# Order edges for the context norm and the second silu row, two more load buffers in the attention, and context rows seven pieces apart

## The chip, the cores and the metric

The kernel runs on one core of a Trainium2 chip. The core has engines that run at the same time, each through its own list of instructions in order: TensorE (PE in the profile; PEld are its weight loads) multiplies matrices, VectorE (DVE) and ScalarE (ACT) work elementwise, GpSimd (POOL) and SyncE (SP) here mostly start DMA transfers. Transfers run on 16 DMA engines; an engine that starts one goes on at once, and whoever needs the data waits for a semaphore. The metric is the device time of one execution in microseconds (us); lower is better.

## The reference

The kernel computes one block of a diffusion backbone: 512 latent tokens (SEQ) and 256 context tokens, width 2048, everything in fp32. Cut to what matters:

```python
shift, scale, gate       = split(silu(c)     @ w_ada + b_ada)      # for the latent tokens
shift_c, scale_c, gate_c = split(silu(c_ctx) @ w_ada + b_ada)      # for the context tokens
h  = rmsnorm(x,   norm_g) * (1 + scale)   + shift                  # 512 x 2048
hc = rmsnorm(ctx, norm_g) * (1 + scale_c) + shift_c                # 256 x 2048
p  = h @ w_in                                                      # 2048 x 9216: q, k, v, z_a, u_b, z_b, g_a, g_b
kc, vc = heads of hc @ w_in[:, k and v columns]
q, k = rope(rmsnorm(q)) * scale, rope(rmsnorm(k));  kc = rmsnorm(kc)
attn = softmax(q @ [k, kc].T) @ [v, vc]                            # 12 query heads, 4 key heads of 128
y_a  = (attn * silu(z_a)) @ w_proj_a                               # branch A
y_b  = (fourier_mix(u_b) * silu(z_b)) @ w_proj_b                   # branch B
y    = (sigmoid(g_a) * y_a + sigmoid(g_b) * y_b) @ w_out
out  = rmsnorm(x + gate * y, final_g)
```

The context needs a norm over its own rows (256 numbers), a scale and a shift per column, and only then its products with the key and value weights. The gate column of the conditioning, silu(c) @ w_ada, is only used at the very end.

## The kernel before

**Tiling.** Weights come from HBM in pieces of 128x1024 fp32 (512 KB), by DMAs that SyncE starts (L212) into "raw" buffers, tiles named wr. Some products use a sum of weight pieces; GpSimd builds those by accumulating loads into longer-lived chain buffers named R (L215, L280). TensorE multiplies in a reduced fp32 format; to keep precision, each piece is split in two, and every product is three matmuls, hi x hi, hi x lo and lo x hi (`mm3`, L324 to L328). The split is a copy on ScalarE (L176, tiles whi) and a subtraction on VectorE (L177, tiles wlo); smaller splits write tiles named s. Three matmuls by four make the work of one piece, twelve matmuls of 512 columns.

**Stages.** After the norm and the conditioning come eight groups of projections (g = 0 to 7: three for q and z_a, two of gates, one for k and v, two of gates). Each is done with seven products instead of eight, in a Strassen-like scheme, named in the order P1, Q5, P2, Q6, P7, Q3, Q4, with four weight pieces each. The results of products stand in PSUM under the names x, y and banks. Then comes the attention, 48 steps (12 heads by four blocks of 128 queries) plus three that run out. In each step TensorE computes scores, VectorE takes the row maximum (L1274), ScalarE the exponential (L1276), TensorE turns the probabilities (L1292) and multiplies them with the values. Branch B's products run between these as a "filler", with weight pieces called pab. GpSimd meanwhile builds sums of branch weights (`weight_sum`, from L1410 on). Branch A and the output projection follow.

**Buffers.** There are four raw buffers (`RAW`, pool `wp`), and up to two more in pool `rp` and two in pool `gvp` at times; the list `raw_pools` says which pools a load may use, and `load_more` starts loads, in order, as long as one is free. The two of `gvp` lie over an older area, the tile qr, in which normalised and rotated queries and keys are put together before they are stored (qz_d at L976, k_d at L986); the context norm's diagonals, the context rows and their forms (`cparts`, stored in cf_d) use the same tile. Whoever writes that area waits until the stores that read it are done. In the attention, tiles of 128x1024 (probabilities, queries and others) come from a list of 32 freed slots, by `take` and `give`.

**The context.** In groups 3 and 4 the pieces carry extra work, by the number n, which counts pieces from group 3 on: `context_piece` (L72) says at which n the squares of the context tokens ("cn") and a context row ("cr", `context_row`) are done. The `context_norm` (L1055) is one of the jobs called after a piece; it makes two diagonal matrices of the inverse norms (L1060), and `context_spread` (L1063), three jobs later, spreads them over the partitions with a matmul and copies them into qr (L1066). Each of the four rows multiplies its tokens with gain and norm on VectorE (L1075), forms sums (L1078, L1084) and stores them (cf_d).

**The conditioning's gate.** The row silu(c) is made in two halves (`load_row`, `silu_of_row`): a tanh on ScalarE (L1101) into a scratch tile e, then one VectorE operation (L1102). `use_gate` (L1107) multiplies 32 pieces of gate weights with it, each in a raw buffer that is free again afterwards. The first half of the row serves gates 0 to 15, the second 16 to 31; gates from number 16 on are all used in the attention.

**What sets the order.** The program is written in one sequence, and a scheduler of the tile framework puts each engine's instructions in an order from dependencies and its own estimates. `tc.issue_after(i)` adds an edge: what is issued under it stands behind instruction i. Nothing else fixes where a small operation without such an edge stands among the splits on ScalarE and VectorE.

Of the kernel before, what the change touches and what calls it, by code (L numbers as in the profile page):

```python
# [10 lines left out]
F32 = mybir.dt.float32  # L11
F32R = mybir.dt.float32r
ACT = mybir.ActivationFunctionType
ALU = mybir.AluOpType
# [4 lines left out]
P = 128  # L19
# [8 lines left out]
NKEY = T + C  # L28
# [37 lines left out]
NQZ, KV = 3, 5  # L66
# [6 lines left out]
def context_piece(g, name, pc):  # L73

    n = 28 * (g - NQZ) + 4 * ONE_GROUP.index(name) + pc
    if n % 2 == 0 and 0 <= n < 8:
        return "cn", n // 2
    if n % 8 == 2 and 18 <= n < 50:
        return "cr", n // 8 - 2

# [37 lines left out]
def block_kernel(ctx, tc, xT, ctx_rows, ctx_toks, x, c_row, w_ss, w_gate, vecs, qkg, rope, dft_c, dft_s,  # L120
                 w_start, w_g, w_pab, w_o, final_g, out):
    nc = tc.nc
# [29 lines left out]
    def uid(s):  # L152
        cnt[0] += 1
        return f"{s}{cnt[0]}"
# [25 lines left out]
    todo, ahead = [], []  # L180
    chain, left = [], [0] * 4
    raw_pools, hl_pools = [(wp, RAW, "raw", RAW)], [wp] * HL
# [40 lines left out]
    def load_more():  # L223
        while todo and len(ahead) < 8 and may[0] and start_load():
            may[0] -= 1
# [23 lines left out]
    last_split, split_of, in_line = [], [], []  # L249
# [49 lines left out]
    def get_aside(key):  # L299

        while not any(e.key == key for e in ahead):
            assert start_load(), key
        e = next(e for e in ahead if e.key == key)
        ahead.remove(e)
        load_more()
        return e.raws[0][1]


    free, retired, home = [], [], {}
# [4 lines left out]
    def take(shape, dt=F32, pool=None):  # L314
        p = next((p for p in free if p[0] is pool), free[0])
        free.remove(p)
        t = slot_tile(p, shape, dt)
        home[id(t)] = p, t
        return t

    def give(*ts):
        free.extend(home.pop(id(t))[0] for t in ts)
# [8 lines left out]
    ident = const.tile([P, P], F32, name="ident")  # L331
# [75 lines left out]
    for g in range(LAST + 1):  # L407
        for name in ONE_GROUP:
# [6 lines left out]
            for pc in range(4):  # L415
                p = context_piece(g, name, pc)
# [4 lines left out]
            for pc in range(4):  # L421
                if (g, name, pc) in GATE_AT:
                    q = GATE_AT[g, name, pc]
                    stream(("gate", q), w_gate[q], 1024, 1, "raw")
                    e = todo.pop()
# [227 lines left out]
    rp = ctx.enter_context(tc.tile_pool(name="rp", bufs=1, reuse_waits="tile"))  # L653
# [19 lines left out]
    raw = get(("dftc", 0))  # L673
# [374 lines left out]
    crs, diag = qr[:, 1792:], qr[:, :256].rearrange("p (b c) -> p b c", b=2)  # L1048
# [5 lines left out]
    def context_norm():  # L1054

        ss = sums[:, 4:6]
        nc.vector.tensor_tensor(ss, sums[:, 0:4:2], sums[:, 1:4:2], op=ALU.add)
        root_of(ss, D)
        for b in range(2):
            nc.vector.tensor_scalar(diag[:, b, :], ident, ss[:, b : b + 1], None, op0=ALU.mult)  # L1060

    def context_spread():
        acc = pair("y")[:, 0, :C]  # L1063
# [34 lines left out]
    def silu_of_row(half, e):  # L1098

        row = crow[half]  # L1100
        nc.scalar.activation(e, row, ACT.Tanh, scale=0.5)  # L1101
        nc.vector.scalar_tensor_tensor(row, e, 1.0, row, op0=ALU.add, op1=ALU.mult)  # L1102
# [36 lines left out]
    for g, kind in enumerate(KINDS):  # L1139
        if g == 3:  # L1140
            jobs += [lambda: None] * 12 + [context_norm, lambda: None, lambda: None, context_spread]
        elif g == KV:
            while jobs:
                job()
            assert not any(p[2] == "raw1" for e in ahead for p, _ in e.raws)
        elif g == KV + 1:
            qzs.close()
            gvs, gvp = region("gvp", "right", reuse_waits="tile")
            hl_pools += range(MORE_HL)
        group = Group(g, forms, new_ev, {"qz": qz_done, "kv": kv_done, "gate": gate_done}[kind], {"a": "x", "b": "y", "c": "x"})  # L1150
        if g == KV:
            group.more = Context()
        for name in ONE_GROUP:
            if (g, name) in ((0, "Q4"), (KV + 1, "P1")):
                assert not any(p[2] == "raw0" for e in ahead for p, _ in e.raws)
                load_row(int(g > 0))
            elif (g, name) == (1, "Q5"):
                silu_of_row(0, flat(new_ev()))
            elif (g, name) == (KV + 1, "Q3"):
                silu_of_row(1, gvp.tile([P, 1024], F32, tag="raw", bufs=2, name=uid("e")))  # L1160
            if (g, name) == (0, "P7"):
                raw_pools.remove((rp, 1, "raw0", 1))
            if (g, name) == (0, "Q5"):
                hl_pools += range(MORE_HL)
            elif (g, name) == (0, "P2"):

                with tc.issue_after(last_split[-1][1].ins):
                    rotations(HD ** -0.5)
            elif (g, name) == (KV, "P1"):
                load_rotations(qkg[:, 2:4, :])  # L1170
            elif (g, name) == (KV, "Q5"):
                rotations(1.0)
            elif (g, name) == (KV - 1, "Q3"):
                raw_pools.remove((rp, 1, "raw1", 1))
                hl_pools[:] = [p for p in hl_pools if not isinstance(p, int)]
            elif (g, name) == (KV + 1, "Q6"):
                raw_pools.append((rp, 1, "raw1", 1))
            elif (g, name) == (KV + 1, "Q4"):
                raw_pools.append((gvp, 2, "raw", 2))
            elif (g, name) == (LAST, "P7"):  # L1180
                raw_pools.remove((gvp, 2, "raw", 2))
            elif (g, name) == (LAST, "Q3"):

                free += [(fms[i], f"s{i}") for i in (4, 5, 6, 7, 12, 13, 14, 15, 8, 9, 10, 11, 2, 3, 0, 1)]
                for h in range(2):
                    load_head(h)
            elif (g, name) == (LAST, "Q4"):
                hl_pools[:] = [p for p in hl_pools if not isinstance(p, int)]
                get_keys(0)
                jobs.append(lambda: turn_queries(0, pair("y")[:, 0, :]))  # L1190
            group.run(name)
# [61 lines left out]
    def fill(n):  # L1253
        for _ in range(n):
            next(fl, None)

    probs, pts, AT, A1, A2 = {}, {}, {}, {}, {}
    bf = {f: [None] * 6 for f in ("A11", "A12", "A22") + FORMS}
    bheld = {}
    NSTEP = 4 * NH  # L1260
    maxima = [None]

    def scores(i):
        h, t = divmod(i, 4)
        kh, kl = kv[h // GQ][:2]
        s = slice(t * P, (t + 1) * P)
        qh, ql = qs[h][:, 0, s], qs[h][:, 1, s]
        sc = next_wide()

        m = 512 if sc is not wide[1] else 256  # L1270
        for a, b in ((0, m), (m, NKEY)):
            mm3(sc[:, a:b], qh, ql, kh[:, a:b], kl[:, a:b], True, True)
        mx = stats[:, 4 * (i % 4) : 4 * (i % 4) + 4]
        maxima[0] = nc.vector.tensor_reduce(mx[:, 0:1], sc[:, :NKEY], axis=AX.X, op=ALU.max, negate=True)  # L1274
        probs[i] = take((NKEY,))
        nc.scalar.activation(probs[i], sc[:, :NKEY], ACT.Exp, bias=mx[:, 0:1], accum_out=mx[:, 1:2])  # L1276
        if t == 3:
            give(qs.pop(h))

# [139 lines left out]
                       lambda: nc.gpsimd.dma_start(p7_d[i, pc], t)))  # L1419

    summed = []
    fill(2)
    filled = 2
    a_groups = []
    for i in range(NSTEP + 3):
        h, t = divmod(i, 4)
        if i < NSTEP:
            if t == 2 and h + 2 < NH:
                load_head(h + 2)
            if i % 12 == 10 and i // 12 + 1 < NKV:  # L1430
                get_keys(i // 12 + 1)
            scores(i)
        want = min(3 + 61 * (i + 1) // NSTEP, 64) + (i == NSTEP - 1)
        if want > filled:
            fill(1)
            filled += 1
        if i % 2 == 0 and i >= 4:
            values((i - 4) // 2)
        if 1 <= i <= NSTEP:
            turn(i - 1)  # L1440
            divide(i - 1)
        if t == 1 and h + 1 < NH:
            turn_queries(h + 1, b1())
        if want > filled:
            fill(want - filled)
            filled = want
        if 10 <= i < 28:
            n, step = divmod(i - 10, 3)
            if step == 0:
                weight_sum(n)  # L1450
            else:
                summed[-1][step]()
            if step == 2:
                give(summed.pop()[0])
        if i in GATE_STEPS:
            n = NGATE + GATE_STEPS.index(i)
            use_gate(n, get_aside(("gate", n)), maxima[0])
            if n == 2 * KK - 1:
                raw_pools.append((rp, 1, "raw0", 1))
        for q, name in {43: [(0, "Z5"), (0, "S3")], 44: [(0, "S2")], 45: [(0, "S4")], 47: [(1, "Z5")], 48: [(1, "S3")],  # L1460
                        49: [(1, "S2"), (1, "S4")]}.get(i, ()):
            branch_forms(q, name)
        if i == NSTEP - 1:
            a_groups.append(a_group(0))
            first = a_groups[0].steps("P1")
        if NSTEP > i - 2 >= NSTEP - 3:
            next(first)
            next(first)
# [321 lines left out]
```

## Time and profile before

| what | us |
|---|---|
| median of three runs | 1318.34 |
| lowest, highest run | 1317.89, 1322.4 |
| the profiled execution's own time | 1329.0 |
| its span | 1327.0 |
| TensorE busy | 1290.2 (97%) |
| VectorE busy | 994.9 (75%) |
| ScalarE busy | 683.9 (52%) |
| GpSimd busy | 180.8 (14%) |
| TensorE's clock, mean over the span | 0.99 |

The profile is one execution taken by the hardware profiler; its time is 10.7 us above the median of the runs without one. In rows of the timeline the columns are the start in us from the span's start, the duration in us, engine, line, operation, what it writes <- what it reads, and in brackets how long the engine stood idle before it and who ended that. A row of the waits gives the waiting group, whom it waited for, the total, the number of times and the longest. A row of the windows gives a stretch, its length, the busy time of PE, PEld, DVE, ACT and POOL with their counts, TensorE's granted clock, the share of the DMA engines and GB/s. An engine name with a q (SPq, ACTq) is that engine's DMA starts, where an x behind the tile is the number of DMAs grouped in the row.

### The profile page before, as it was taken

To read this page: it belongs to the slowest core of one execution; us is meant where nothing else is said; L and a number is where in the kernel's file an instruction comes from. 1 tells how busy PE (TensorE), PEld (TensorE's weight loads), DVE (VectorE), ACT (ScalarE), POOL (GpSimd) and SP (SyncE) were. 2 spreads that over 40 slices of the span, in tenths; PEclk is the share of its full clock that TensorE was granted. 3 is DMA by queue.
4 is the path that set the end of the run, shared out by engine and by line. 5 is a ranking of instruction groups with operands and counts; after the bars stand their busy time and mean duration, and the time that the engine had idled before them with its cause. 6 is when DMAs were issued, how large, how long until landed. Compare 5 with 4: busy or idle time off the path is not lost.

```text
span 1327.0 us, 17532 instructions
## 1 busy us (share of the span) xinstructions
PE 1290.2 (97%) x6522; PEld 1053.7 (79%) x6522; DVE 994.9 (75%) x1295; ACT 683.9 (52%) x1079; POOL 180.8 (14%) x244
## 2 busy tenths in 40 slices
PE   7999999999998999999999999998999999999997
PEld 3577888888887887788887888787888888878885
DVE  4666899988687776758686666686888867787676
ACT  5222655545455544544354554665666645464544
POOL 0110011110102110011021020121000312121210
PEclk9999999999999999999998999998999999999999
DMA  9898587987898879977867897678563799998985
GB/s 385 336 366 330 178 243 201 243 237 251 197 313 231 242 248 277 297 205 187 281 194 220 288 225 260 200 232 251 181 201 120 210 241 245 253 207 221 224 209 173
DMA packets 103718, 318.54 MB, mean 240 GB/s; under 512 B 9808, under 2 KB 33104, under 8 KB 99280
## 3 DMA queue, kind: packets, MB, share of 16 engines
q0 software_dynamic: 30288, 123.75, 39.3%
q1 hardware_dynamic: 48720, 163.65, 34.7%
q10 hardware_dynamic: 24624, 30.02, 6.6%
q8 instruction: 51, 0.84, 0.2%
q14 instruction: 35, 0.29, 0.1%
HBM read 283.30 MB, written 34.09 MB: 239 GB/s over the span
## 4 chain that ended last, share of the span: by engine, by line
PE 69%; DMA 15%; DVE 9%; ACT 4%; issue 3%; POOL 0%; ACTq 0%; SPq 0%; DVEq 0%; POOLq 0%
PE banks L326 9%; PE banks L327 9%; PE banks L328 9%; PE x L327 6%; PE x L328 6%; PE x L326 6%; PE y L327 4%; PE y L326 4%; PE y L328 4%; DMA s<-in_w_pab 3%; DVE wlo L177 3%; DMA wr<-in_w_g 2%; PE pd L531 2%; DMA cf_d<-qr 2%; DVE s L177 2%
## 5 line engine op out<-in xcount | busy, mean ns | idle before, releaser
L176 ACT ACTIVATE whi<-R 128x1024 fp32r<-128x1024 f32 x138 | 144.9, 1057 | 135.2 <-PE banks L328 44.2
L177 DVE TENSOR_TENSOR wlo<-R,whi 128x1024 fp32r<-128x1024 f32 x138 | 167.4, 1220 | 53.3 <-ACT whi L176 53.2
L177 DVE TENSOR_TENSOR wlo<-wr,whi 128x1024 fp32r<-128x1024 f32 (+1 forms) x123 | 148.3, 1211 | 64.9 <-ACT whi L176 64.8
L176 ACT ACTIVATE whi<-wr 128x1024 fp32r<-128x1024 f32 (+1 forms) x123 | 128.7, 1051 | 120.2 <-PE y L328 34.1
L326 PE MATMUL banks<-whi,s 128*128 128x512 f32 x396 | 157.4, 397 | 1.9 <-DVE ev L859 1.5
L327 PE MATMUL banks<-wlo,s 128*128 128x512 f32 x396 | 155.9, 394 | 0.8 <-DVE wlo L177 0.8
L328 PE MATMUL banks<-whi,s 128*128 128x512 f32 x396 | 155.1, 392 | 0.0
L327 PE MATMUL x<-wlo,s 128*128 128x512 f32 x352 | 138.2, 393 | 4.5 <-DVE wlo L177 4.5
L328 PE MATMUL x<-whi,s 128*128 128x512 f32 x352 | 138.0, 392 | 0.0
L326 PE MATMUL x<-whi,s 128*128 128x512 f32 x352 | 137.9, 392 | 0.0
L327 PE MATMUL y<-wlo,s 128*128 128x512 f32 x316 | 123.6, 391 | 1.2 <-DVE wlo L177 1.2
L326 PE MATMUL y<-whi,s 128*128 128x512 f32 x316 | 123.8, 392 | 0.4 <-DVE cxe L1012 0.4
L328 PE MATMUL y<-whi,s 128*128 128x512 f32 x316 | 123.3, 391 | 0.0
L280 POOL DMA_DIRECT2D R<-in_w_g x64 | 55.9, 874 | 435.3 <-DVE wlo L177 253.2
L176 ACT ACTIVATE s<-wr 128x512 fp32r<-128x512 f32 (+2 forms) x93 | 60.4, 676 | 71.5 <-DMA wr<-cf_d 20.1
L177 DVE TENSOR_TENSOR s<-wr,s 128x512 fp32r<-128x512 f32 (+2 forms) x93 | 66.9, 748 | 38.7 <-ACT s L176 38.6
L326 PEld LDWEIGHTS banks<-whi,s 128*128 128x128 f32 x396 | 74.6, 188 | 17.4 <-ACT s L176 1.9
L328 PEld LDWEIGHTS banks<-whi,s 128*128 128x128 f32 x396 | 74.5, 188 | 15.5
L327 PEld LDWEIGHTS banks<-wlo,s 128*128 128x128 f32 x396 | 74.6, 188 | 15.3 <-DVE wlo L177 1.5
L327 PEld LDWEIGHTS x<-wlo,s 128*128 128x128 f32 x352 | 66.6, 189 | 19.2 <-DVE wlo L177 5.3
L328 PEld LDWEIGHTS x<-whi,s 128*128 128x128 f32 x352 | 66.6, 189 | 13.8
L326 PEld LDWEIGHTS x<-whi,s 128*128 128x128 f32 x352 | 66.5, 189 | 13.9
(293 smaller groups left out, 2839.3 us busy)
## 6 DMA issues: line engine op xcount, KB each, us to landing
wr<-in_w_g SPq DMA_DIRECT2D x128, 512.0 KB, 4.8
R<-in_w_g POOLq DMA_DIRECT2D x64, 512.0 KB, 6.7
wa<-in_w_ss POOLq DMA_DIRECT2D x26, 1024.0 KB, 7.9
R<-in_w_g SPq DMA_DIRECT2D x32, 512.0 KB, 5.8
wr<-in_w_gate SPq DMA_DIRECT2D x32, 512.0 KB, 4.4
wr<-in_w_o SPq DMA_DIRECT2D x24, 512.0 KB, 7.4
R<-in_w_o POOLq DMA_DIRECT2D x24, 512.0 KB, 8.6
wr<-in_w_pab SPq DMA_DIRECT2D x20, 512.0 KB, 5.3
```

Of the source, the lines that this page charges most:

```text
L176: first = nc.scalar.activation(hi, src, ACT.Copy)
L177: return first, nc.vector.tensor_tensor(lo, src, hi.bitcast(F32), op=ALU.subtract)
L280: nc.gpsimd.dma_start(chain[e.pc], e.nxt, accum_op=ALU.add)
L326: nc.tensor.matmul(o, ah, bh, start=start, stop=False, skip_group_check=cont)
L327: nc.tensor.matmul(o, ah, bl, start=False, stop=False, skip_group_check=cont)
L328: nc.tensor.matmul(o, al, bh, start=False, stop=stop, skip_group_check=cont)
L531: last = nc.tensor.matmul(acc[32 * j : 32 * j + 32, :256], c2[:, 8 * h + k, :], w[:, k, :], start=n < 4, stop=n >= KK - 4)
```

## The change

- Context rows: the pieces after which a row is handled are n = 18, 25, 32 and 39 instead of 18, 26, 34 and 42.
- The two diagonals of the context norm get an order edge behind the VectorE half of the last split.
- The second half of silu(c) is no longer made in group 6 at Q3, with its scratch tile e in the `gvp` area; it is made in step 3 of the attention with a slot from the list, under order edges behind that step's maximum and exponential. For that, `maxima` also keeps the exponential.
- The two buffers of `gvp` join the list of load buffers at (6, Q6) rather than (6, Q4), in one statement with the one of `rp`. Q6 stands two products ahead of Q3 and three ahead of Q4 in the order of a group.
- Ahead of the attention two of the 32 slots become load buffers (`more_raw`). At step 33 they leave the list again and go back to the slots once the pieces in them are used; `get_aside` now returns such slots as well, as `get` did.

```diff
@@ def context_piece
-    if n % 8 == 2 and 18 <= n < 50:
-        return "cr", n // 8 - 2
+    if n % 7 == 4 and 18 <= n < 46:
+        return "cr", n // 7 - 2
@@ def get_aside
         ahead.remove(e)
+        free.extend(p[0::2] for p, _ in e.raws if p in retired)
         load_more()
@@ def context_norm
-        for b in range(2):
-            nc.vector.tensor_scalar(diag[:, b, :], ident, ss[:, b : b + 1], None, op0=ALU.mult)
+        with tc.issue_after(last_split[-1][1].ins):
+            for b in range(2):
+                nc.vector.tensor_scalar(diag[:, b, :], ident, ss[:, b : b + 1], None, op0=ALU.mult)
@@ the groups
-            elif (g, name) == (KV + 1, "Q3"):
-                silu_of_row(1, gvp.tile([P, 1024], F32, tag="raw", bufs=2, name=uid("e")))
...
             elif (g, name) == (KV + 1, "Q6"):
-                raw_pools.append((rp, 1, "raw1", 1))
-            elif (g, name) == (KV + 1, "Q4"):
-                raw_pools.append((gvp, 2, "raw", 2))
+                raw_pools += [(rp, 1, "raw1", 1), (gvp, 2, "raw", 2)]
@@ the attention
-    maxima = [None]
+    maxima = [None, None]
...
-        nc.scalar.activation(probs[i], sc[:, :NKEY], ACT.Exp, bias=mx[:, 0:1], accum_out=mx[:, 1:2])
+        maxima[1] = nc.scalar.activation(probs[i], sc[:, :NKEY], ACT.Exp, bias=mx[:, 0:1], accum_out=mx[:, 1:2])
...
     summed = []
+    more_raw = [(p, 1, t, 1) for p, t in (free.pop(), free.pop())]
+    raw_pools += more_raw
     fill(2)
...
+        if i == 3:
+            with tc.issue_after(maxima[0].ins), tc.issue_after(maxima[1].ins):
+                e = take((1024,))
+                silu_of_row(1, e)
+                give(e)
+        if i == 33:
+            for p in more_raw:
+                raw_pools.remove(p)
+                retired.append(p)
+                if not any(r is p for a in ahead for r, _ in a.raws):
+                    free.append(p[0::2])
         if i in GATE_STEPS:
```

## The prediction

> **What bounds the kernel now.** I read the page's busy shares and slices first, to see which engine is the bound and where it is not; then the waits of TensorE, which name each stretch in which the bound stands still; then the timelines of the engines around the three longest of these.
>
> ```profile
> span 1327.0 us, 17532 instructions
> PE 1290.2 (97%) x6522; PEld 1053.7 (79%) x6522; DVE 994.9 (75%) x1295; ACT 683.9 (52%) x1079; POOL 180.8 (14%) x244
> PEclk9999999999999999999998999998999999999999
> ...
> PE x L327 <- DVE wlo L177: 4.5, 2, 3.6
> PE banks L1292 <- ACT s L1276: 3.7, 1, 3.7
> PE x L326 <- ACT s L176: 3.2, 1, 3.2
> ```
>
> TensorE is busy for 97% of the span and none of its instructions is changed, so nothing can be won except where it stands still or runs slowly. The waits (total, times, longest) name three stops of over 3 us behind the start. The first of them in the matmul timeline (start, duration):
>
> ```profile
> 423.29 0.39 PE L328 MATMUL x<-whi,s 128*128 128x512 f32 x1
> 423.52 0.39 PE L326 MATMUL x<-whi,s 128*128 128x512 f32 x1
> 427.50 0.79 PE L327 MATMUL x<-wlo,s 128*128 128x512 f32 x1 [3.59 <-DVE wlo L177]
> ...
> 433.21 0.58 PE L328 MATMUL x<-s,s 128*128 128x512 f32 x1
> 433.63 0.39 PE L326 MATMUL x<-s,s 128*128 128x512 f32 x1
> 433.86 0.40 PE L327 MATMUL x<-s,s 128*128 128x512 f32 x1
> ```
>
> Before the stop and from 433.63 on matmuls start every 0.23 us; the 14 between start every 0.43 us. The wait thus costs twice: the stop, and some 6 us at half clock behind it (so do the two others; a shorter one, at 836 us below, does not). From 423.52 to 433.63 are 15 starts, 3.4 us at full pitch; they took 10.1, so **stop 1 costs 6.7 us**.
>
> **The change part by part.** The engines' orders of the two kernels, set side by side, have equal counts of instructions; TensorE's order is the same up to the attention, and there too it only shifts turns and fills slightly.
>
> *The two diagonals (L1060).* They write into the qr area, which earlier stores still read.
>
> ```profile
> 416.96 1.12 ACTq L976 DMA_DIRECT2D qz_d<-qr  x2
> 417.99 1.22 DVE L177 TENSOR_TENSOR wlo<-wr,whi 128x1024 fp32r<-128x1024 f32 x1
> 426.02 0.28 DVE L1060 TENSOR_SCALAR qr<-ident,small 128x128 f32<-128x128 f32 x1 [6.82 <-DMA qz_d<-qr]
> 426.23 1.22 DVE L177 TENSOR_TENSOR wlo<-wr,whi 128x1024 fp32r<-128x1024 f32 x1
> 451.69 0.35 ACT L1066 COPY qr<-y 128x256 f32<-128x256 f32 x1
> ```
>
> VectorE stood 6.82 us before the first diagonal for a store issued at 416.96; the split queued behind it (426.23) is the one that stop 1 waits for. In the changed order the diagonals stand behind splits which in the time of before run at about 438 us, 12 us after the store has landed, so they wait for nothing; what needs them (ones times diagonal, then the copy at 451.69) is 13 us later. The split can run at 419.2, four microseconds ahead of TensorE. Worth −6.7; 0 if something else holds the split. The order edge itself adds a wait on a split of VectorE's own queue, 0; without that cover it would hold at most one split (1.22).
>
> *Context rows seven pieces apart (L78).* The numbers 18, 26, 34, 42 become 18, 25, 32, 39. In SP's order one row load passes two weight loads; VectorE's sixteen multiplications (L1075) keep their places to within a few instructions. A row loaded sooner and used as before holds one of four buffers longer. The rows and their area end in this place:
>
> ```profile
> L1075 DVE SCALAR_TENSOR_TENSOR qr<-wr,gain,qr x16: 475/479/484, 455.4 to 512.4; 128x256 f32<-128x256 f32 x16
> 524.73 1.29 DVE L934 SCALAR_TENSOR_TENSOR qr<-qr 128x512 f32<-128x512 f32 x2 [1.31 <-DMA qr<-in_qkg]
> 525.95 0.39 PE L326 MATMUL x<-whi,s 128*128 128x512 f32 x1
> 527.21 0.50 PE L327 MATMUL x<-wlo,s 128*128 128x512 f32 x1 [0.87 <-DVE wlo L177]
> 420.00:560.00 140.00, 134.33 (x580) 109.86 (x579) 100.72 (x145) 68.36 (x95) 10.39 (x12) 0.98 0.86 265
> ```
>
> The chain through the rows to the rotations (L934) costs TensorE 1.0 us at 526 (1.26 less one pitch). If it ends a little sooner, −1.0; if it ends later by as much as the next loads are late, up to the 5.5 it takes to make this a full stop like 1. The table row (busy of five engines, clock, DMA share 0.86) says the transfers have little room here. I take +0.5: the order of VectorE, which sets the chain, hardly moves.
>
> *The second silu (L1101, L1102) moved into step 3 of the attention.*
>
> ```profile
> 691.94 1.07 ACTq L986 DMA_DIRECT2D k_d<-qr  x2
> 707.33 0.39 PE L328 MATMUL x<-s,s 128*128 128x512 f32 x1
> 709.27 1.06 ACT L1101 ACTIVATE e<-crow 128x1024 f32<-128x1024 f32 x1 [9.72 <-DMA k_d<-qr]
> 710.90 0.79 PE L326 MATMUL x<-s,s 128*128 128x512 f32 x1 [3.19 <-ACT s L176]
> 711.49 1.22 DVE L1102 SCALAR_TENSOR_TENSOR crow<-e,crow 128x1024 f32<-128x1024 f32 x1
> 716.91 0.40 PE L327 MATMUL y<-wlo,s 128*128 128x512 f32 x1
> ```
>
> ScalarE waited 9.72 us to write e over an area that a store issued at 691.94 still read; the split behind it is what TensorE waits for from 707.33. From there to 716.91 are 14 starts, 3.2 us at full pitch, in 9.6: **stop 2 costs 6.4 us**. The move takes the wait away. SP's loads into the same area still wait for that store, but the first piece they bring is used after 720 us. In the attention the 1.06 us on ScalarE and 1.22 on VectorE stand beside other work (table below: 81% and 66% busy), tied behind the maximum and the exponential of a step, whose wait is over by then: 0, at most their 2.3 us. Later use of that area for loads (Q6 for Q4's list entry) is part of this: 0.
>
> *Two more load buffers in the attention, until step 33.*
>
> ```profile
> 836.00:1050.00 214.00, 208.22 (x1355) 182.12 (x1354) 172.89 (x281) 141.23 (x270) 28.39 (x46) 0.98 0.62 191
> 862.50 0.33 SPq L212 DMA_DIRECT2D wr<-in_w_pab  x1
> 893.76 10.88 SPq L212 DMA_DIRECT2D wr<-in_w_pab  x2
> 902.31 0.28 PE L327 MATMUL banks<-ptl,s 128*128 128x256 f32 x1
> 901.97 1.06 ACT L176 ACTIVATE whi<-wr 128x1024 fp32r<-128x1024 f32 x1 [3.62 <-DMA wr<-in_w_pab]
> 906.29 0.69 PE L1292 MATMUL banks<-ident,s 128*128 128x128 f32 x2 [3.70 <-ACT s L1276]
> 906.30:911.50 5.20, 5.20 (x18) 4.60 (x19) 4.08 (x9) 2.67 (x6) 1.36 (x3) 0.50 0.93 298
> ```
>
> The load of 893.76 could only be issued when the gate multiplication on VectorE had freed its buffer, and took 8.2 us to ScalarE's start at 901.97; ScalarE stood there 3.62 us with the exponential of the step queued behind, and TensorE 3.7 us from 902.31, then 5.2 us at clock 0.50. Of these 5.2, seven 256-column starts at 0.21 instead of 0.12 and six of 512 columns at 0.43 instead of 0.23 make about 1.9: **stop 3 costs 5.6 us**. In the changed order this piece is loaded some 20 us sooner: −5.6.
>
> The buffers shift the scarcity, they don't end it. Counted in the time between the release of a buffer and TensorE's need, before has four pab loads with under 12 us (the stop's own has 11.6, with 3.1 to the issue, 8.2 to the landing and 4.3 of splits and reduction after); the changed order has two, of 11.0 and 8.0 us. The load at 862.50 had 11.0 as well and cost nothing. So with a quick transfer each costs 0, and with one like 893.76's each is a full stop of 5.6. I take 2.5 for both together, ends 0 and 11.2.
>
> [...]
>
> **Sum**, on the profiled execution: −6.7 + 0.5 − 6.4 − 5.6 + 2.5 = −15.7 of its 1329.0. The runs without a profile have a median of 1318.34, 10.7 us less. What these 10.7 are no view shows. All three stops end on transfers; if those are quicker without the profiler by that much together, only 5.0 of the 15.7 are there to win. Between 5.0 and 15.7 I take a little over the middle, 11.5, since the stops are the only long ones yet the 10.7 can lie anywhere in 1329: 1318.3 − 11.5 = **1307 us**.
>
> **The rivals.**
>
> *The stops are shorter without the profiler.* A stop of 1.9 us leaves no half clock behind it:
>
> ```profile
> 835.99 0.39 PE L328 MATMUL x<-whi,s 128*128 128x512 f32 x1
> 837.85 0.47 PE L326 MATMUL banks<-whi,s 128*128 128x512 f32 x1 [1.47 <-DVE ev L859]
> 838.15 0.40 PE L327 MATMUL banks<-wlo,s 128*128 128x512 f32 x1
> ```
>
> The three are 3.2 to 3.7 us idle; one microsecond less of transfer each may leave three stops of 2.5 and no slow stretch, 7.5 in all, less the same 3.0 of new costs: 1314. For it: the 10.7 us. Against: the runs of before agree within 0.4%. [...]
>
> *Two new stops in the attention.* Both tight loads collide with GpSimd's sums, 11.2 instead of 2.5: 1307 + 8.7 = 1316. For it: DMA share 0.93 behind stop 3. Against: 0.62 over the attention, and the load of 862.50.
>
> *The rows' chain (slower).* A row holding a buffer for two more pieces makes weight loads late where the DMA share is 0.86. Each stop of 1 us there that passes 3 us becomes one like stop 1, +5.5; the four rows and the rotations at 526 make five places, up to +27, and from about three of them on (16) the gain is gone; with all five 1307 + 27 = 1334, with four 1329. Against: only one row load moves, past two weight loads.
>
> *The change misses its stops.* Another wait holds split and silu where the old one did, and only stop 3 goes: 1318.3 − 5.6 + 3.0 = 1316.
>
> **How the numbers follow.** No change that a measurement could tell is 0.5%, 6.6 us: 1311.7 to 1324.9. The sum as given, 1300 to 1311: 0.62, all faster. Shorter stops: 0.14, a third of it faster. Two new stops: 0.08, same. Missed stops: 0.05, same. Rows' chain: 0.11, slower. Faster 0.62 + 0.05 = 0.67, same 0.22, slower 0.11. The range leaves out the slower rival's far part and what lies below −18.7: 1300 to 1322.
>
> **What would show it.** Right: no wait before the diagonals, wlo of that piece at about 419; no idle at 707; clock 0.50 nowhere between 420 and 920; pab loads in the attention issued 20 us sooner. Wrong: a stop of over 3 us at 526 or 546, or one at about 870 to 930 waiting for a pab piece behind ScalarE's copy; or stops gone and the median unmoved, which would put the profile's stops down to the profiler.

## The result, and the profile after

The changed kernel's median is 1312.46 us (9 executions, 1309.96 to 1315.62). In the comparisons made with it the kernel before has 1324.22 us (9 executions, 1317.89 to 1327.70). The ratio is **0.992, 95% interval 0.9898 to 0.9943**: by the ratio 10.6 us or 0.8% faster (the medians differ by 11.8). A second comparison gave 0.9929 (0.9903 to 0.9954). The three executions of before that the prediction started from, with a median of 1318.34, were quick ones: over 57 later executions its median is 1325.1.

The changed kernel's page, its waits of TensorE (total, times, longest), its windows (length; busy PE, PEld, DVE, ACT, POOL; clock; DMA share; GB/s) and two groups of its code lines:

```profile
span 1310.7 us, 17551 instructions
PE 1281.5 (98%) x6522; PEld 1046.7 (80%) x6522; DVE 995.5 (76%) x1295; ACT 685.8 (52%) x1079; POOL 183.3 (14%) x244
PEclk9999999999999999999999999999999999999999
...
PE x L328 <- DVE wlo L177: 2.9, 3, 2.1
PE banks L327 <- DVE ev L860: 1.5, 1, 1.5
...
420.00:560.00 140.00, 136.75 (x603) 112.15 (x602) 104.46 (x148) 69.44 (x95) 10.38 (x12) 1.00 0.88 274
836.00:1050.00 214.00, 212.23 (x1378) 185.44 (x1377) 178.30 (x284) 143.85 (x270) 33.11 (x52) 1.00 0.66 201
...
L1062 DVE TENSOR_SCALAR qr<-ident,small x2: 285/286/288, 433.6 to 433.8; 128x128 f32<-128x128 f32 x2
L1103 ACT ACTIVATE s<-crow x1: 1057/1057/1057, 840.2 to 840.2; 128x1024 f32<-128x1024 f32 x1
```

Among the long waits behind the start, none of the three stops is left, and the clock of both windows is 1.00 where it was 0.98. The diagonals (now L1062) run at 433.6 without a wait, the silu row (now L1103) at 840.2 in the attention without one. Of the new stops the longest is this one, at the key rotations (now L935):

```profile
519.89 1.29 DVE L935 SCALAR_TENSOR_TENSOR qr<-qr 128x512 f32<-128x512 f32 x2 [2.04 <-DMA qr<-in_qkg]
519.86 0.39 PE L327 MATMUL x<-whi,s 128*128 128x512 f32 x1
522.38 0.50 PE L328 MATMUL x<-wlo,s 128*128 128x512 f32 x1 [2.13 <-DVE wlo L177]
```

Set side by side by matmul number (both kernels have 6522), the two profiled executions differ by this much in each stretch of before's time:

| stretch of before | what lies there | difference, us |
|---|---|---|
| up to 420 | nothing changed | −0.3 |
| 420 to 449 | stop 1 | −6.75 |
| 449 to 701 | rows, key rotations, k and v | +2.2 |
| 701 to 730 | stop 2 | −6.45 |
| 730 to 1000 | attention, stop 3 | −5.4 |
| to the last matmul | branch and output products | −0.1 |

That is −16.8 between two profiled executions, against −10.6 between the kernels. Each execution also has its mean granted clock on record, and this explains a part of the gap. Time by clock, over 57 executions of before and 16 of the changed kernel:

| mean clock | before: executions, mean us | changed: executions, mean us |
|---|---|---|
| up to 0.991 | 8, 1329.7 | none |
| 0.992 and 0.993 | 15, 1327.6 | none |
| 0.994 and 0.995 | 29, 1323.9 | 4, 1316.5 |
| 0.996 and above | 5, 1320.6 | 12, 1312.6 |

The execution of before in the profile, at 0.990, is of a rare kind: three of the 57 are that low. On the mean the clock went from 0.9935 to 0.9968; of a span of some 1318 us this is 4.2 us of lost full clock less (the part below 1, times the span). In a row of equal clock the kernels still differ by 7 to 8 us. I put that down to the time for which TensorE stood still less; the table does not show it by itself.

### The profile page after: what moved, and what is told of

Same layout as the page of the kernel before. It is cut to its first block, busy times and chain, and to the rows that moved or that the text cites. A ratio compares the mean times of both kernels' runs of the same rounds, so it can differ in the third digit from the quotient of the medians.

```text
span 1310.7 us, 17551 instructions
## 1 busy us (share of the span) xinstructions
PE 1281.5 (98%) x6522; PEld 1046.7 (80%) x6522; DVE 995.5 (76%) x1295; ACT 685.8 (52%) x1079; POOL 183.3 (14%) x244
## 4 chain that ended last, share of the span: by engine, by line
PE 73%; DMA 10%; DVE 9%; issue 3%; ACT 3%; SPq 0%; POOL 0%; ACTq 0%; DVEq 0%
PE banks L327 10%; PE banks L328 10%; PE banks L329 9%; PE x L329 6%; PE x L328 6%; PE x L327 6%; PE y L328 5%; PE y L329 5%; PE y L327 5%; DMA wr<-in_w_g 4%; DVE wlo L177 3%; PE pd L532 2%; PE banks L1290 2%; PE pb L327 2%; DVE s L177 2%
```

## The experiments

### Each part alone

Four kernels, each the kernel before with one part of the change. The diagonals:

```diff
-        for b in range(2):
+        with tc.issue_after(last_split[-1][1].ins):
+            for b in range(2):
```

> Only the order edge on the two diagonals. Theory (each part removes one stop, and the stop is the same without the profiler): stop 1 and its slow stretch gone, 6 to 7 us less in the profile and in the timed runs; the stops at 707 and 902 stay, each with a slow stretch. Rival (the stops are long only under the profiler): the profile loses 6 to 7 us, the timed runs at most 3. Rival (the time comes back later, at the rows' chain): the stop at 526 grows by 1 us or more and the profile loses 5 or less.

Measured: 0.9974 (0.9953 to 0.9994), 3.4 us faster; the profiled span is 4.7 shorter. Stop 1 is gone, the other two stand, and a third has grown in the timeline of TensorE:

```profile
519.67 0.39 PE L326 MATMUL x<-whi,s 128*128 128x512 f32 x1
523.38 0.50 PE L327 MATMUL x<-wlo,s 128*128 128x512 f32 x1 [3.31 <-DVE wlo L177]
...
523.30:530.10 6.80, 6.72 (x22) 5.38 (x23) 6.80 (x9) 4.34 (x6) 1.72 (x2) 0.75 1.01 273
```

The stop at the key rotations went from 1.26 us to 3.71 (start to start), with 0.75 of the clock over the 6.8 us behind it: the second rival of this run came true. The chain to the rotations ends in the load of the key gains, which is issued behind the landing of the last store of the rows (in before the store starts at 517.26 and takes 3.55 us to land, and the load is issued at 521.24). First the kernel before, then the one with the diagonals' edge:

```profile
521.24 0.41 ACTq L929 DMA_DIRECT2D qr<-in_qkg  x1
```

```profile
515.52 0.41 ACTq L929 DMA_DIRECT2D qr<-in_qkg  x1
520.89 1.29 DVE L934 SCALAR_TENSOR_TENSOR qr<-qr 128x512 f32<-128x512 f32 x2 [3.22 <-DMA qr<-in_qkg]
```

TensorE comes there 6.3 us sooner (519.67 for 525.95) and the load is issued 5.7 us sooner, but from its issue to the rotations it takes 5.4 us where it took 3.5 (to 524.73). So of the 2.4 us that are given back there, 1.9 are the load's.

The silu row, with the buffers of that area joining one product earlier:

```diff
-            elif (g, name) == (KV + 1, "Q3"):
-                silu_of_row(1, gvp.tile([P, 1024], F32, tag="raw", bufs=2, name=uid("e")))
...
+        if i == 3:
+            with tc.issue_after(maxima[0].ins), tc.issue_after(maxima[1].ins):
+                e = take((1024,))
+                silu_of_row(1, e)
+                give(e)
```

> Only the second silu row moved into the attention, with the load buffers of that area joining one product earlier as in the change. Theory: stop 2 (707) gone, 6 to 6.5 us less in profile and timed runs, no new wait in step 3 of the attention. Rival (profiler): the timed runs lose at most 3.

Measured: 0.9955 (0.9931 to 0.9978), 6.0 us faster. No stop of over 0.5 us stands between 640 and 830, and none in step 3 of the attention. The profiled span is 4.7 us shorter, less than the theory's 6 to 6.5: stop 1 is longer in that execution, 5.51 us.

The two load buffers:

```diff
+    more_raw = [(p, 1, t, 1) for p, t in (free.pop(), free.pop())]
+    raw_pools += more_raw
...
+        if i == 33:
+            ...
```

> Only the two more load buffers in the attention. Theory: stop 3 (902) gone, new small waits on the two tight pab loads of 0 to 2 us in all: 3.5 to 5.6 us less in profile and timed runs. Rival (the scarcity only moves): a new stop of over 3 us in the attention, no gain.

Measured: 0.9966 (0.994 to 0.9991), 4.5 us faster. In its profile the attention, from 836 us on, has no stop of over 0.5 us. The profiled span is 10.3 us shorter, more than this part can be worth: stop 1 happens to be 1.50 us there.

The spacing of the rows:

```diff
-    if n % 8 == 2 and 18 <= n < 50:
-        return "cr", n // 8 - 2
+    if n % 7 == 4 and 18 <= n < 46:
+        return "cr", n // 7 - 2
```

> Only the context rows seven pieces apart. Theory: VectorE's order barely changes, within 1 us of before. Rival (rows' chain): a row holds a load buffer for longer, the stops at 526 and 546 grow, 2 to 6 us more than before.

Measured: 1.0017 (0.9994 to 1.004). Between 1 us less and 5 us more; no gain is to be seen, a small loss is not excluded. The rival's sign is in the profile, a stop of 2.76 us at the rotations where before has 1.26, but TensorE also came there 2.7 us sooner (523.25) in that execution, where no slow clock followed stop 1 (1.00 over the 6.8 us behind it).

The four differences, by their ratios, sum to −11.7 us, the whole change gives −10.6. They do not add up so neatly as that looks, as the next runs show.

### The change without a part

The change itself once more, on the chip of the three kernels below:

> The whole change once more, beside the three variants of it on the same chip. Theory (the parts add up): the edges, the silu row and the buffers alone measured 3.4, 6.0 and 4.5 us less and the rows 2.2 more, so 11 to 12 us less than before, mean clock 0.997 or 0.998 in most runs. Rival (the profiled 16 us are the true gain): 15 to 17 us less.

Measured: 0.9929 (0.9903 to 0.9954), 9.4 us faster, clock 0.995 in three executions of seven and 0.997 or 0.998 in four. The profile's 16 us are excluded.

Without the spacing (rows eight apart again, otherwise the change):

> The change without its seven-piece spacing of the context rows (eight again). Theory from the rows alone (2 us slower): 1 to 3 us faster than the change. Rival (with the first stop gone TensorE comes sooner to the rotations, so the rows have to come sooner too, and the spacing pays): the stop at the rotations grows from 2.5 us to 3.5 us or more, with half clock in part of the runs, 1 to 4 us slower than the change.

Measured: 0.9914 (0.989 to 0.9937). The stop at the rotations did grow, as the rival said, to 4.40 us in the profile (519.21 to 523.61), but the executions without the spacing are no slower than the change: by the ratios 2.0 us faster, as the theory has it too, which is within the intervals. The spacing neither pays nor costs anything that these runs can tell.

Without the load buffers:

> The change without the two load buffers in the attention. Theory (parts add up): a stop of 3 to 4 us near 885, 4 to 5 us slower than the change. Rival (the order of the attention alone, shifted by the silu row, removes that stop): within 1.5 us of the change.

Measured: 0.9919 (0.989 to 0.9948): as fast as the change, within an interval of some 4 us each way. So the 4.5 us that the buffers are worth alone are not seen any more once the other parts are in. And without both, with only the diagonals' edge and the silu row's move:

> Only the diagonals' edge and the silu row's move, rows eight apart and no more buffers. Theory (the change without buffers was as fast as the change, and the rows' spacing pays nothing): 9 to 11 us less than before, the whole gain of the change; stop 3 at about 1 to 2 us without a slow stretch in most runs. Rival (the buffers and the spacing carry their part): 3 us or more slower than the change, that is 7 us less than before or worse.

Measured: **0.9901 (0.9876 to 0.9926)**, the whole gain of the change from two of its parts, as far as these runs can tell. (The kernel before was slower in this comparison, 1328.07, so the medians say more than the ratio: 1313.88 here, 1312.46 and 1314.86 for the change.)

Why the buffers no longer matter is seen in the load that made stop 3. Its place in the order is the same in all kernels without the buffers, and in the five that have the stop it is issued 8.2 to 8.6 us before the last matmul ahead of the stop. What differs is when GpSimd's weight sums are issued around it (SPq and POOL starts; first the kernel before, then the one with two parts), and how long it takes:

```profile
890.42 0.88 POOL L1418 DMA_DIRECT2D s<-in_w_pab  x1 [1.12 <-DMA s<-in_w_pab]
892.93 0.88 POOL L1418 DMA_DIRECT2D s<-in_w_pab  x1 [1.63 <-DMA s<-in_w_pab]
DMA to landing us min/median/max: 8.2/8.2/8.2
```

```profile
884.03 6.69 SPq L212 DMA_DIRECT2D wr<-in_w_pab  x2
885.25 0.88 POOL L1415 DMA_DIRECT2D s<-in_w_pab  x1 [6.10 <-DMA s<-in_w_pab]
886.51 0.88 POOL L1415 DMA_DIRECT2D s<-in_w_pab  x1 [0.38 <-DMA s<-in_w_pab]
DMA to landing us min/median/max: 3.6/3.6/3.6
```

In before the load (893.76) comes just after two accumulating transfers; in the two-part kernel just ahead of them. Over six kernels that load without extra buffers, by time to landing:

| kernel | load issued, against the two transfers | load to landing, us | TensorE's stop, start to start, us |
|---|---|---|---|
| before | behind both | 8.2 | 3.98 |
| diagonals alone | between them | 7.4 | 3.25 |
| rows alone | behind both | 7.2 | 3.05 |
| silu alone | between them | 6.7 | 2.87 |
| change without buffers | between them | 5.8 | 1.95 |
| diagonals and silu | ahead of both | 3.6 | none |

Where there is a stop, it is the landing time less some 4 us (3.8 to 4.2). That the order of issue decides the landing is argued from these rows, one execution each; no run moved GpSimd's sums by themselves.

### The stop at the key rotations

The longest new stop is the one at 520. The change, with the key rotations tied as the diagonals are:

```diff
             elif (g, name) == (KV, "Q5"):
-                rotations(1.0)
+                with tc.issue_after(last_split[-1][1].ins):
+                    rotations(1.0)
```

> The change, with the key rotations tied behind a split in the way of the diagonals. Theory (that stop is the chain through stores of the rows and the load behind them, which does not get shorter when TensorE does): the 2.5 us stop at 520 goes, 2 to 4 us faster than the change. Rival: the keys are then late for their store or for the piece behind, and a stop of the same size stands 10 to 30 us later.

Measured: 0.9933 (0.991 to 0.9957), no gain. The rival was right:

```profile
538.87 0.39 PE L329 MATMUL y<-s,s 128*128 128x512 f32 x1
540.13 0.49 PE L327 MATMUL y<-whi,s 128*128 128x512 f32 x1 [0.87 <-ACT whi L176]
542.25 0.80 PE L328 MATMUL y<-wlo,s 128*128 128x512 f32 x1 [1.63 <-DVE wlo L177]
```

520 has no stop of over 1 us any more; two stand at 539 to 542, 3.4 us together, and 6.8 us of slow clock follow them. With the rows eight apart too:

> The change with rows eight apart and the key rotations tied behind a split. Theory: the stop at 519 (4.4 us with rows eight apart) goes, and a stop of 1 to 3 us comes near 540 in its place; within 2 us of the change. Rival (the two edits help each other): 3 us or more faster than the change.

Measured: 0.9903 (0.9881 to 0.9924), 3.6 us of stops at 539 to 542 again, within the spread of the change. No version beats the change by more than the runs can tell; the two-part kernel reaches it with less.

### How much cover the moved diagonals have

The change, with the diagonals written several times over (`for b in list(range(2)) * 13`, and `* 22`), to make a stop of known length.

> The change with the two diagonals written thirteen times each (24 more instructions of 0.24 us on VectorE, the same values): a stop of known size at 436. VectorE comes 5.8 us later to a split that TensorE needs 4.3 us after it: a stop of about 1.5 us, no slow stretch, 1 to 2.5 us slower than the change, clock as in the change.

> The same with twenty-two times each (42 more, 10.1 us): a stop of about 5.8 us. Theory (whether a stop of this length costs one or two slow windows of 3.4 us depends on where the window stands): mean clock lower by 0.0013 or 0.0026 in the runs, 7.5 to 9.5 us slower than the change. Rival (half clock always follows for a fixed time): all runs lower by 0.0026, 9 us or more. Rival (the rows' chain gives it back, since TensorE comes later to the stop at 520): 6 us or less slower.

Measured: 0.991 (0.989 to 0.9931) and 0.9912 (0.9891 to 0.9932): neither is slower than the change by the ratios. The change itself did not run beside them; the two variants that did (the two-part kernel and the one just above) have medians of 1313.88 and 1313.41, these two 1315.09 and 1315.21, so a loss of 1 or 2 us is not excluded, and one of 7.5 is. Of the three theories for the second the first two missed. The third's bound, 6 us or less, holds, but it supposed a stop that did not come, and the first run's stop of 1.5 us did not come either. The second's profile, in which the stop at the rotations is 3.87 us:

```profile
435.20 8.72 DVE L1062 TENSOR_SCALAR qr<-ident,small 128x128 f32<-128x128 f32 x44
...
442.44 0.39 PE L329 MATMUL y<-s,s 128*128 128x512 f32 x1
443.78 0.71 PE L1067 MATMUL y<-qr,ones 128*128 128x128 f32 x4 [0.95 <-DVE qr L1062]
444.25 0.48 PE L327 MATMUL x<-s,s 128*128 128x512 f32 x1
```

VectorE is held for 8.7 us, and TensorE stops for 1.3, and that for the diagonals themselves, not for the splits behind them. I had counted 4.3 us of cover; there are some 8. So where the edge put them, VectorE can be held for 8.7 us at the price of a stop of 1.3, while at the old place a wait of 6.8 us was stop 1. The question of what a stop of 6 us costs stays without a run of its own.

## Why the prediction was right

The direction, the size (−11.5 forecast, −10.6 measured) and the time (1307 forecast, 1312.5 measured, within 1300 to 1322) held; the 5.5 us between forecast and time come from the quick first three executions of before (median 1318.34, where nine have 1324.22). By its steps:

- **Stop 1, −6.7.** −6.75 in the profiles, but only 3.4 us alone in the timed runs: 2.4 us of it come back at the key rotations.
- **Rows and rotations, +0.5.** Mis-sized: +2.2 in the profiles, 1.3 of it the stop at 520 (1.26 to 2.52 us). The prediction took VectorE's order for what sets the chain. In the run with the diagonals alone the rows did come sooner with TensorE, and it was the load of the key gains that took 5.4 us instead of 3.5; in the changed kernel's profile it takes 4.2. The slower rival's place was right, its reason (a row holding a buffer for longer) was not shown.
- **Stop 2, −6.4.** −6.45, and 6.0 alone in the timed runs. It holds best; the moved silu costs nothing that any row shows.
- **Stop 3 and the buffers, −5.6 + 2.5.** Together −5.4 in the profiles, better than −3.1. Of the two tight loads, put at 2.5 us together, one causes a stop, 0.78 us idle at 868.83, behind a split whose load ScalarE waits for (the 0.40 us at 865.17 stand in the two-part kernel too, at 866.88):

```profile
865.14 1.06 ACT L176 ACTIVATE whi<-wr 128x1024 fp32r<-128x1024 f32 x1 [1.62 <-DMA wr<-in_w_pab]
867.77 0.28 PE L329 MATMUL banks<-pth,s 128*128 128x256 f32 x1
868.83 0.44 PE L1129 MATMUL banks<-ident,wr 128*128 128x128 f32 x2 [0.78 <-DVE ptl L177]
```

  But the prediction gave the whole of this to the buffers. They do remove the stop alone, and the two-part kernel is rid of it without them: with the other stops gone the load stands ahead of GpSimd's sums in its profile (in that of the change without buffers it stands between them, with 1.95 us of stop left). That a stop could go because two transfers change places in time is in none of its steps.
- **From 15.7 to 11.5.** The number was right and its reason only half. The prediction put the gap down to transfers that are quicker without the profiler; no run shows them to be. What the runs show is that the profiled execution of before was one with more slow clock than nearly all others: three stretches of 6.8 us, 20.5 us in all. The mean clock of the 57 executions, 0.9935, makes 17 us of slow clock in a span of 1323, of which some 6 belong to the stretch at the end, behind the last matmul (5.9 us at 0.50 in the profile of before, 4.6 in that of the changed kernel); that leaves some 11, about half of the 20.5. Two stops of nearly one length that differ in this stand in the last section. The rival of the shorter stops, which has no slow stretch behind any of the three, gave 1314; the measured 1312.46 lies between it and the forecast.
- **The rivals.** Two new full stops in the attention: no. The change misses its stops: no. Slower by the rows' chain: no, though that is where the gain was given back.

## What to carry to other kernels

Look for an operation that waits for a store with work queued behind it: here the diagonals waited 6.82 us and the silu 9.72, and the splits behind them left TensorE idle for 3.59 and 3.19. Put behind work that is due anyway, both ran without a wait, and these two moves were the whole gain that the runs can tell. When a stop is taken away, look at the next place where the bound engine meets a chain of transfers: if that chain does not come sooner by as much, it hands part of the gain back (2.4 us at the key rotations, with the diagonals alone). A profile is one execution: stops of 2.13 and 2.18 us differed here in whether half clock followed, so read the clock of many executions before pricing the slow stretches from one.

## What the runs showed of the hardware

Stops of nearly one length differed here in whether half clock followed. This is the stop at the rotations in two executions of the changed kernel, the profiled ones of the first and of the second comparison, each with stretches of 3.41 us around it (behind the length stands the busy time of PE, the clock is the third number from the end):

```profile
522.38 0.50 PE L328 MATMUL x<-wlo,s 128*128 128x512 f32 x1 [2.13 <-DVE wlo L177]
517.58:520.99 3.41, 2.67 (x12) 1.88 (x10) 1.36 (x3) 1.66 (x3) 1.39 (x2) 1.00 0.99 274
520.99:524.40 3.41, 2.02 (x9) 1.67 (x10) 3.41 (x5) 0.00 (x0) 0.00 (x0) 1.00 1.03 198
```

```profile
523.82 0.63 PE L328 MATMUL x<-wlo,s 128*128 128x512 f32 x1 [2.18 <-DVE wlo L177]
520.63:524.04 3.41, 1.23 (x6) 0.73 (x5) 2.70 (x4) 0.01 (x1) 0.00 (x0) 1.00 1.03 200
524.04:527.45 3.41, 3.41 (x9) 2.64 (x9) 3.41 (x5) 1.25 (x3) 0.81 (x1) 0.50 1.05 205
```

Behind 2.13 us idle the clock stayed at 1.00, behind 2.18 us it was 0.50 for 3.41 us. In the profile of before the three slow stretches behind stops are 6.83 us long each, and the full-speed stretches between them 276.5 and 187.7 us, 81 and 55 times 3.41. The rows above are marked off in steps of 3.41 us from a slow stretch of the same profile (in the first execution back from the one at its end, at 1306.06). So marked, the stop of the first execution lies in two of these stretches, with 0.7 and 1.4 us idle; in the second all of its 2.18 us lie in one. Two more stops, marked in the same way: with the rows alone 3.09 us lie in two stretches, 1.9 and 1.2, and no slow clock followed (1.00 from 425.9 to 432.7); in the two-part kernel 2.17 of 2.27 us lie in one stretch, and the next has 0.50:

```profile
425.89 0.50 PE L327 MATMUL x<-wlo,s 128*128 128x512 f32 x1 [3.09 <-DVE wlo L177]
421.28:424.69 3.41, 1.52 (x7) 0.94 (x5) 0.28 (x2) 1.64 (x2) 0.00 (x0) 1.00 1.01 355
424.69:428.11 3.42, 2.22 (x10) 1.81 (x11) 3.42 (x6) 0.00 (x0) 0.00 (x0) 1.00 0.34 103
```

```profile
523.73 0.50 PE L327 MATMUL x<-wlo,s 128*128 128x512 f32 x1 [2.27 <-DVE wlo L177]
521.56:524.97 3.41, 1.24 (x5) 1.05 (x6) 3.41 (x6) 0.00 (x0) 0.00 (x0) 1.00 1.01 179
524.97:528.38 3.41, 3.41 (x9) 2.67 (x8) 3.41 (x5) 2.27 (x4) 1.56 (x2) 0.50 1.01 286
```

The three stops of before have 2.87, 2.37 and 2.06 us idle in one of these stretches and 0.72, 0.81 and 1.64 us in the next; from that next one on the clock was 0.50 for two stretches each time. So of these seven stops slow clock followed the five with 2.06 to 2.87 us idle in one stretch, and neither of the two with 1.4 and 1.9 us at most. No run settles what decides it.

The store that stop 1 waits for took nearly the same time in each execution, 8.9 to 9.3 us to landing in the four profiles in which that edge is missing. The stop is 1.50 us (buffers alone), 3.48 us (rows alone), 3.98 us (before) and 5.51 us (silu alone), as the store is issued 9.0, 7.1, 6.6 and 5.0 us ahead of the matmul before the stop. What moves the issue no run here shows. The load of the key gains did take a different time, 3.5 us from issue to the rotations in before and 6.1 in the change with rows eight apart. Neither wait had one price in these runs: 1.50 to 5.51 us at stop 1, and 1.26 (before) to 4.40 us (rows eight apart) at the rotations, start to start.
